# A transformer block with a recurrent time mix: when its weight chunks are loaded and split, where y is transposed, and the form of its recurrence

## The chip, the cores and the metric

One core of a Trainium2 chip runs the whole kernel. The metric is the device time of one execution in microseconds; the median of three runs is quoted. The five engines that take part are TensorE (PE), VectorE (DVE), ScalarE (ACT), GpSimd (POOL) and SyncE (SP), which issues most of the DMAs. Each runs its own instructions in the order in which they were recorded and waits for the others by semaphores.

## The reference

One layer, 1024 tokens of width 1024, all in float32:

```python
x = x + 0.5 * swiglu(rms_norm(x, ffn1_norm), ffn1_w_gate, ffn1_w_up, ffn1_w_down)
z = rms_norm(x, mix_norm) @ w_in
z_rwkv, z_attn, z_gate = jnp.split(z, [RWKV_COLS, RWKV_COLS + ATTN_COLS], axis=-1)
y_rwkv = rwkv7_time_mix(z_rwkv, ...)
y_attn = dilated_attention_mix(z_attn, cos, sin, q_norm, k_norm)
g_rwkv, g_attn = jnp.split(jax.nn.sigmoid(z_gate), N_BRANCHES, axis=-1)
x = x + (g_rwkv * (y_rwkv @ w_br_rwkv) + g_attn * (y_attn @ w_br_attn)) @ w_out
x = x + 0.5 * swiglu(rms_norm(x, ffn2_norm), ffn2_w_gate, ffn2_w_up, ffn2_w_down)
x = x + jax.nn.sigmoid(rms_norm(x, ple_norm) @ ple_w_gate) * (p_i @ ple_w_proj)
```

The change touches the time mix and the attention's beginning. The time mix shifts z by one token, makes r, k, v, a decay w, a rate a and a gate g of it, and runs, for each of 8 heads of 64, a state of 64 x 64 through the 1024 tokens: `state = state * w + sa (kk * a) + v k`, with `sa = -state kk`, and `y = state r`. y is then normalised per head, gets a bonus term and is multiplied by g. The attention has three groups of four heads, each with its own window and dilation.

## The kernel before, in words

Every large product is made of three float32r products (`mm3`, L265 to L267), since weights and activations are split into a high and a low part. A weight chunk of 128 x 1024 is loaded by `wchunk` (L252 to L260): a DMA into a staging tile `wst` (two buffers), then ScalarE writes the high part of a `wsp` tile (three buffers; L249) and GpSimd the low part (L250). All users of the mixer draw on these two rings in turn.

The mixer (`mixer`, L1872) has two stages. In the first, `rwkv` (L845), the time mix goes through 8 units: 4 pairs of heads, each in two halves of 512 tokens. A unit has three steps, written as generators:

- `zstage` (L922): three z blocks (k, r, v) of 24 dense products each; each begins with its own `zw` chunk.
- `wkv_a` (L968), `wkv_b` (L1140): decay and keys (`QR`, `BK`), scores of keys with keys and queries (L1055), the inverse of a triangular matrix in blocks (`X` on VectorE, L1119 and L1121; L1182 to L1212 on TensorE), then a recurrence over 8 chunks of 64 tokens. A step of it (L1247 to L1266) makes two products of QR with the state S (L1254, one per head, 64 x 64), a subtraction on VectorE (L1258), two products with BKn (L1263), and a state update on VectorE (L1264).
- `wkv_c` (L1282): y out of the accumulators (`psy`, whose last products are L1278), its norm (`rsqrt`, L237 to L243, small operations of VectorE), gain, bias and bonus on GpSimd (L1319 to L1324), the product with g on VectorE (L1326), then four transposes on TensorE (L1329) and the store of y (L1332).

In the second stage the queries and keys of a head group are normalised and rotated (`qk_post`, L1474), then the attention core runs (`attn_core`, L1544): per block of 128 queries the scores (L1575), mask and maximum on VectorE (L1579), the exponentials on ScalarE (L1585), transposes (L1597) and the products with v (L1618).

What sets the order is `weave` (L112): it records the instructions of several streams into one program by a simple clock of its own. A stream tells with each `yield` how long its piece keeps TensorE busy and how long it then has to wait, as `yield 0, 8.0` ahead of y's transposes (L1325). Streams marked "F" are dense products, which fill the gaps: first `zstage`, then a filler of gate blocks (`gates`, L1350) and the first attention projection (`qkv_first`, L1430). What of the filler is not used up in the first stage goes on in the second, beside `qkv_gemm` (L1440), whose next projection waits until `qk_post` is done with the last.

## Time and profile before

| what | us |
|---|---|
| median of 3 runs | 2735.73 |
| lowest and highest run | 2727.03, 2739.34 |
| the profiled execution, its own time | 2731.04 |
| its span, first to last instruction | 2729.3 |
| TensorE busy in the span | 2518.9 (92%) |
| VectorE, ScalarE, GpSimd busy | 1586.2, 973.2, 1148.3 |
| mean granted clock of TensorE | 0.961 |

A busy time is the time in which an engine had an instruction in work. TensorE's instructions overlap, so its busy time is not all work at its peak. The granted clock is the share of the full TensorE clock that the chip allowed. A float32 product on TensorE stands in the trace as two passes, a float32r product and a transpose as one.

### The profile page before, as it was taken

Reading aid. Unit: us, or ns where it says so; the run is one execution under the profiler, and the core shown is the slowest. Engines: PE = TensorE matmul, PEld = TensorE weight load, DVE = VectorE, ACT = ScalarE, POOL = GpSimd, SP = SyncE. Lnnn points to the kernel's source line nnn. Section 1 sums busy time; section 2 is a strip of 40 time slices with the busy share of each in tenths; the row PEclk is TensorE's granted clock in tenths of the full one; section 3 lists DMA queues with packets and bytes.
Section 4 is the critical chain, followed back from the end, with each engine's and each line's share of the span. In section 5 each row is a group of like instructions: output and inputs, shape, how many; then the busy total and the mean of one; then the engine's idle time right before and its main releaser. Section 6 shows DMA issues by size and latency. Waiting matters only on the chain.

```text
span 2729.3 us, 37026 instructions
## 1 busy us (share of the span) xinstructions
PE 2518.9 (92%) x14541; PEld 2038.0 (75%) x14541; DVE 1586.2 (58%) x2519; ACT 973.2 (36%) x1700; POOL 1148.3 (42%) x635
## 2 busy tenths in 40 slices
PE   6899999899999999889989998879799999989899
PEld 5688888777777666667877998658578888768677
DVE  4865556788715555554356325382876556677852
ACT  5433333333434323332224343421533332333541
POOL 2675556555424333332222212150565655555540
PEclk9899999999999999999989999899899999999999
DMA  5222222736333222222231101572132222453532
GB/s 187 93 85 70 93 78 93 282 120 211 129 117 91 60 62 56 62 60 59 76 113 43 63 32 43 180 210 113 46 99 82 88 77 93 147 222 110 180 121 93
DMA packets 272498, 289.18 MB, mean 106 GB/s; under 512 B 46282, under 2 KB 202540, under 8 KB 272068
## 3 DMA queue, kind: packets, MB, share of 16 engines
q1 hardware_dynamic: 264932, 274.59, 30.7%
q10 hardware_dynamic: 7392, 12.23, 1.3%
q8 instruction: 114, 1.87, 0.3%
q14 instruction: 60, 0.49, 0.1%
HBM read 222.64 MB, written 64.14 MB: 105 GB/s over the span
## 4 chain that ended last, share of the span: by engine, by line
PE 48%; DVE 13%; POOL 3%; issue 2%; DMA 2%; ACT 2%; SPq 0%; ACTq 0%; DVEq 0%; POOLq 0%
PE g L265 7%; PE g L266 6%; PE g L267 6%; PE dn L266 6%; PE dn L267 6%; PE dn L265 5%; PE tr L267 1%; PE tr L265 1%; PE tr L266 1%; POOL wsp L250 1%; PE t L1055 1%; PE s L1575 1%; DMA fb<-f 1%; DVE sub L1119 1%; PE pt L1597 1%
## 5 line engine op out<-in xcount | busy, mean ns | idle before, releaser
L250 POOL TENSOR_TENSOR wsp<-wr,wsp 128x1024 fp32r<-128x1024 f32 (+1 forms) x158 | 361.5, 2296 | 374.4 <-ACT wsp L249 334.2
L250 POOL TENSOR_TENSOR wsp<-wst,wsp 128x1024 fp32r<-128x1024 f32 x71 | 173.4, 2445 | 425.2 <-ACT wsp L249 372.4
L250 POOL TENSOR_TENSOR wsp<-ws,wsp 128x1024 fp32r<-128x1024 f32 x88 | 222.0, 2524 | 212.0 <-ACT wsp L249 210.3
L265 PE MATMUL g<-h,wsp 128*128 128x512 f32 x496 | 220.7, 445 | 12.2 <-DVE h L1714 10.6
L265 PE MATMUL g<-wsp,h 128*128 128x256 f32 (+1 forms) x664 | 217.0, 327 | 16.0 <-ACT raw L1427 10.2
L267 PE MATMUL g<-wsp,h 128*128 128x256 f32 (+1 forms) x664 | 207.6, 313 | 0.0
L266 PE MATMUL g<-wsp,h 128*128 128x256 f32 (+1 forms) x664 | 207.5, 313 | 0.0
L267 PE MATMUL g<-h,wsp 128*128 128x512 f32 x496 | 201.3, 406 | 0.0
L266 PE MATMUL g<-h,wsp 128*128 128x512 f32 x496 | 201.0, 405 | 0.0
L407 DVE TENSOR_TENSOR ws<-wr 128x512 f32<-128x512 f32 x56 | 86.6, 1554 | 166.8 <-POOL x L250 165.4
L249 ACT ACTIVATE wsp<-ws 128x1024 fp32r<-128x1024 f32 (+1 forms) x110 | 106.4, 968 | 191.6 <-PE dn L267 74.4
L249 ACT ACTIVATE wsp<-wr 128x1024 fp32r<-128x1024 f32 (+1 forms) x158 | 133.7, 851 | 107.6 <-DVE wr L751 42.5
L265 PEld LDWEIGHTS g<-wsp,h 128*128 128x128 f32 x664 | 138.5, 209 | 28.2 <-ACT raw L1427 10.9
L265 PE MATMUL dn<-wsp,h 128*128 128x512 f32 x360 | 143.8, 405 | 13.5 <-DVE x L792 6.9
L266 PE MATMUL dn<-wsp,h 128*128 128x512 f32 x360 | 143.7, 399 | 7.9 <-POOL wsp L250 7.9
L267 PE MATMUL dn<-wsp,h 128*128 128x512 f32 x360 | 142.1, 396 | 0.7 <-DVE h L250 0.6
L266 PEld LDWEIGHTS g<-wsp,h 128*128 128x128 f32 x664 | 139.0, 209 | 3.7 <-issue 0.2
L267 PEld LDWEIGHTS g<-wsp,h 128*128 128x128 f32 x664 | 138.6, 209 | 3.7
L463 DVE TENSOR_TENSOR act<-act,m 128x512 f32<-128x512 f32 x88 | 130.7, 1485 | 1.4
L265 PEld LDWEIGHTS g<-h,wsp 128*128 128x128 f32 x496 | 96.5, 194 | 44.0 <-DVE h L1714 11.6
L267 PE MATMUL dn<-h,wsp 128*128 128x512 f32 x320 | 124.6, 389 | 0.0
L265 PE MATMUL dn<-h,wsp 128*128 128x512 f32 x320 | 124.5, 389 | 0.0
(467 smaller groups left out, 6604.6 us busy)
## 6 DMA issues: line engine op xcount, KB each, us to landing
wr<-ffn_w_down SPq DMA_DIRECT2D x44, 1024.0 KB
wst<-w_in SPq DMA_DIRECT2D x60, 512.0 KB
wr<-ffn_w_gate SPq DMA_DIRECT2D x44, 512.0 KB
wr<-ffn_w_up SPq DMA_DIRECT2D x44, 512.0 KB
actD<-act SPq DMA_DIRECT2D x44, 512.0 KB
a<-actD SPq DMA_DIRECT2D x12, 1024.0 KB
gate<-gst SPq DMA_DIRECT2D x26, 256.0 KB
wst<-ffn_w_down SPq DMA_DIRECT2D x10, 512.0 KB
```

The costliest lines, as they stand in the source:

```text
L249: nc.scalar.activation(dst[:, 0], src, AF.Copy)
L250: (lo_eng or nc.vector).tensor_tensor(out=dst[:, 1], in0=src, in1=dst[:, 0].bitcast(F32), op=ALU.subtract)
L265: mm(ps, lhsT=l[0], rhs=r[0], start=first, stop=False)
L266: mm(ps, lhsT=l[0], rhs=r[1], start=False, stop=False)
L267: mm(ps, lhsT=l[1], rhs=r[0], start=False, stop=last)
L407: self.nc.vector.tensor_tensor(out=out, in0=R[:, i], in1=R[:, j], op=op)
L463: eng.tensor_tensor(out=a, in0=a, in1=v, op=ALU.mult)
L1055: PE.matmul(psd[h][:, i2, e].rearrange("p (a s) -> p a s", a=2), lhsT=BK[hr, i, 2 * e:2 * e + 2].rearrange("p a s -> p (a s)"), rhs=QR[hr, ...
L1119: V.tensor_tensor(out=pr[:, :s + 1, :n], in0=XT[:, :s + 1, s:s + 1].to_broadcast([64, s + 1, n]), in1=at[:, s:s + 1, s + 1:].to_broadcast( ...
L1575: PE.matmul(ps[h][:, pr, :nk * P], lhsT=qT[hr, pr, j * P:(j + 1) * P], rhs=kT[hr, pr, k0:k0 + nk * P], start=True, stop=True)
L1597: PE.transpose(pt[:, h], S[:, h, kt * P:(kt + 1) * P], self.ident)
```

## The change

- Loads and splits of a weight chunk are two calls now, `wload` and `wsplit`. The staging tiles are `wst0` and `wst1`, the split ones `wsp0`, `wsp1`, `wsp2`, each with one buffer; the z blocks use `wst0` and, in turn, `wz` and `wsp0`, the filler `wst1`, `wsp1` and `wsp2`.
- A z block's load is issued when the block before it begins, and its split stands after the fourth of that block's eight pieces. The filler (`fill`, in place of `qkv_first` and the gates ahead of it) does the same.
- The recurrence's two products of 64 x 64 per head become one of 128 x 128 for both: the state is kept as a block-diagonal tile `Sbd` of 128 x 128, whose off-diagonal blocks are zero. The state update on VectorE becomes two, one for each head. The time that a step is said to take on TensorE is 0.11 in place of 0.16, and its second wait 0.7 in place of 0.5.
- y's product with g, transposes and store come after a wait of 14.0 in place of 8.0.
- The scratch for DMAs is smaller (1024), which frees memory.

```diff
@@ class K
-    def wchunk(self, src, kdim, pool=None, tag="wsp", bufs=3):
...
-        st = self.t(self.wp, [P, 1024], "wst", bufs=2)
-        nc.sync.dma_start(st[:, :n].rearrange("p (k n) -> p k n", k=kdim), src)
-        sp = self.t(pool or self.wp, [P, 2, 1024], tag, dt=F32R, bufs=bufs)
-        self.split(sp[:, :, :n], st[:, :n], lo_eng=nc.gpsimd)
+    def wchunk(self, src, kdim, pool=None, tag=None, bufs=1):
+        return self.wsplit(self.wload(src, kdim), pool, tag, bufs)
+    def wst(self, q=None):
+        if q is None:
+            q = self.wq = 1 - self.wq
+        return self.t(self.wp, [P, 1024], f"wst{q}")
+    def wload(self, src, kdim, q=None):
         n = kdim * src.shape[-1]
+        st = self.wst(q)
+        self.nc.sync.dma_start(st[:, :n].rearrange("p (k n) -> p k n", k=kdim), src)
+        return st, kdim, n
...
+    def wsplit(self, load, pool=None, tag=None, bufs=1):
+        st, kdim, n = load
+        sp = self.t(pool, [P, 2, 1024], tag, dt=F32R, bufs=bufs) if pool else self.wsp(tag)
+        self.split(sp[:, :, :n], st[:, :n], lo_eng=self.nc.gpsimd)
@@ def rwkv: zstage, sz
             for x in (1, 0, 2):
-                W = zw(4 * x + hb)
+                if not zready:
+                    zsplit()
+                W = zready.pop()
+                if zorder:
+                    nextz.append(zload(zorder.pop(0)))
                 d = zt[x, hb, hf] = self.t(sp, [P, HALF], f"z{x}{hf}")
-                yield from zblock(4 * x + hb, W, hf, d)
+                for n, r in enumerate(zblock(4 * x + hb, W, hf, d)):
+                    yield r
+                    if n == 3 and nextz:
+                        zsplit()
...
+        def zsplit():
+            zslots.append(zslots.pop(0))
+            zready.append(self.wsplit(nextz.pop(), *zslots[0]))
@@ def wkv_b
-                for h in range(2):
-                    hr = slice(64 * h, 64 * h + 64)
-                    PE.matmul(pu[ur[e], h, 256:320], lhsT=QR[hr, i, qs], rhs=S[hr, cc], start=True, stop=True)
-                yield 0.16, 0.5
-                SP = self.t(sp, [P, 64], "SP", bufs=2)
+                PE.matmul(U2, lhsT=QR[:, i, 0:2].rearrange("p a s -> p (a s)"), rhs=S[:, cc], start=True, stop=True)
+                yield 0.11, 0.5
+                SP = self.t(sp, [P, P], "SP", bufs=2)
                 A.activation(SP, S[:, cc], AF.Copy, scale=pcol)
                 V.tensor_tensor(out=UV[ur[e], i, e].rearrange("p (h s) -> p h s", h=2),
...
+                PE.matmul(dS, lhsT=BKn[:, i, e], rhs=UV[:, i, e], start=True, stop=True)
                 for h in range(2):
                     hr = slice(64 * h, 64 * h + 64)
-                    PE.matmul(pu[hr, 0, 320:384], lhsT=BKn[:, i, e, hr], rhs=UV[:, i, e, hr], start=True, stop=True)
-                V.scalar_tensor_tensor(out=S[:, cc + 1], in0=pu[:, 0, 320:384], scalar=pcol, in1=SP, op0=ALU.mult,
-                                       op1=ALU.add)
-                yield 0.16, 0.5
+                    V.scalar_tensor_tensor(out=S[hr, cc + 1, hr], in0=dS[hr, hr], scalar=pcol[hr], in1=SP[hr, hr],
+                                           op0=ALU.mult, op1=ALU.add)
+                yield 0.11, 0.7
@@ def wkv_c
-        yield 0, 8.0
+        yield 0, 14.0
         V.tensor_tensor(out=yc, in0=yc, in1=gs, op=ALU.mult)
@@ def mixer
         def fill():
-            yield from take(gates, max(NFIRST - gates0, 0) * 16)
-            yield from self.qkv_first(hT, mx, D_["raw"])
+            yield from self.fill(hT, mx, D_["gate"], D_["raw"], range(gates0, NFIRST))
             done.add("raw0")
-            yield from gates
+            yield from self.gates(hT, mx, D_["gate"], range(NFIRST, 16))
```

Line numbers of the changed kernel are some 40 higher in these parts: its L1097 is L1055 of before, L1233 and L1235 are L1191 and L1193, L1368 is L1329, and L284 to L286 are L265 to L267.

On TensorE, third unit, around the four transposes of y (`yc`): before,

```order
L1182 MATMUL t_1342_8315<-TT_8157,SC_7697 64x32 x4
L265 MATMUL g_8276<-h_864_5453,wsp_8272 128x512
L266 MATMUL g_8276<-h_864_5453,wsp_8272 128x512
L267 MATMUL g_8276<-h_864_5453,wsp_8272 128x512
L1182 MATMUL t_1342_8315<-TT_8157,SC_7697 64x32 x8
L1329 MATMUL t_1343_8340<-cst_p_66,yc_8126 128x128 x4
L1055 MATMUL t_1346_8349<-QR_8252,BK_8253 128x128
```

and now,

```order
L1235 MATMUL t_1357_8392<-TT_8138,N_884_5614 64x32 x2
L284 MATMUL g_8323<-h_868_5475,wsp_1264_7847 128x512
L285 MATMUL g_8323<-h_868_5475,wsp_1264_7847 128x512
L286 MATMUL g_8323<-h_868_5475,wsp_1264_7847 128x512
L1097 MATMUL t_1355_8386<-QR_8294,BK_8295 128x128
L1097 MATMUL t_1356_8387<-QR_8294,BK_8295 128x128
L1368 MATMUL t_1358_8444<-cst_p_66,yc_8212 128x128 x4
```

The transposes stood ahead of all scores of the keys; now six of these and the first part of the inverse stand ahead of them. The count of dense products between the unit's last y product (L1278) and the transposes went from 54 to 57, and to the first scores from 54 to 45.

On VectorE, the same unit, around y's product with g (L1326, third row from the end; in the changed kernel L1365, second from the end): before,

```order
L1318 TENSOR_TENSOR yc_8126<-yc_8126,grsy_8197 128x512
L1016 TENSOR_SCALAR n_1329_8246<-t_1327_8237 128x8
L1017 RECIPROCAL n_1329_8246<-n_1329_8246 128x8
L1014 SCALAR_TENSOR_TENSOR ta_8174<-ta_8174,kk_8214 128x512
L1028 SCALAR_TENSOR_TENSOR BK_8253<-ta_8174,iP_8217 128x4x128
L1030 TENSOR_TENSOR BK_8253<-z_1202_7480,iP_8217 128x4x2x64
L1326 TENSOR_TENSOR yc_8126<-yc_8126,gsl_8123 128x512
L888 SCALAR_TENSOR_TENSOR z_1319_8192<-g_8193,omu_5597,zu_8266 128x512
L1185 TENSOR_TENSOR N_882_5609<-t_1342_8315,cst_r_5592 128x16x16
```

and now,

```order
L1056 SCALAR_TENSOR_TENSOR ta_8225<-ta_8225,kk_8240 128x512
L243 SCALAR_TENSOR_TENSOR grsy_8263<-grsu_8264,grsy_8263 128x8
L1072 TENSOR_TENSOR BK_8295<-z_1195_7395,iP_8243 128x4x2x64
L1070 SCALAR_TENSOR_TENSOR BK_8295<-ta_8225,iP_8243 128x4x128
L1357 TENSOR_TENSOR yc_8212<-yc_8212,grsy_8263 128x512
L1365 TENSOR_TENSOR yc_8212<-yc_8212,gsl_8209 128x512
L1227 TENSOR_TENSOR N_884_5614<-t_1351_8356,cst_r_5597 128x16x16
```

The two operations that make BK stand ahead of both large operations on y now (in two other units of before, y's product stood ahead of them).

On TensorE, at the end of the first attention core, where its statistics (`ast`) are transposed: before,

```order
L1597 MATMUL pt_12578<-cst_p_66,S_12528 128x128 x4
L267 MATMUL g_12524<-h_860_5431,wsp_12396 128x512
L1553 MATMUL pt_12588<-cst_p_66,ast_11991 8x128 x4
L1618 MATMUL po_12437<-PT_12571,vt_11726 64x128
L1553 MATMUL pt_12594<-cst_p_66,ast_11991 8x128 x4
L1618 MATMUL po_12437<-PT_12571,vt_11726 64x128 x3
L1618 MATMUL po_12438<-PT_12571,vt_11726 64x128 x4
L265 MATMUL g_12524<-h_862_5442,wsp_12396 128x512
L266 MATMUL g_12524<-h_862_5442,wsp_12396 128x512
L267 MATMUL g_12524<-h_862_5442,wsp_12396 128x512
```

and now,

```order
L285 MATMUL g_12694<-wsp_1965_12664,h_809_5021 128x256
L1671 MATMUL pt_12588<-cst_p_66,S_12544 128x128 x4
L1627 MATMUL pt_12595<-cst_p_66,ast_12122 8x128 x4
L1692 MATMUL po_12478<-PT_12581,vt_11857 64x128
L1692 MATMUL po_12479<-PT_12581,vt_11857 64x128
L1627 MATMUL pt_12601<-cst_p_66,ast_12122 8x128 x4
L1692 MATMUL po_12478<-PT_12581,vt_11857 64x128 x3
L1692 MATMUL po_12479<-PT_12581,vt_11857 64x128 x3
L1589 MATMUL pt_12645<-cst_p_66,rt_1956_12621 128x128 x4
```

The gate products (128 x 512) between and behind the core's steps are gone; products of the next projection (128 x 256) stand between its last steps.

## Rows read from the trace of the kernel before

**Rows 1.** Busy time by stretch: us, then each engine's, granted clock, DMA share, GB/s.
```profile
812.00:1403.00 591.00, 546.40 (x5255) 417.46 (x5256) 301.13 (x720) 187.10 (x378) 193.03 (x154) 0.94 0.24 66
1403.00:1442.00 39.00, 28.08 (x181) 26.69 (x182) 29.10 (x60) 9.93 (x17) 8.37 (x4) 0.82 0.41 137
1442.00:1528.00 86.00, 80.81 (x485) 60.36 (x486) 41.13 (x122) 38.20 (x101) 18.62 (x8) 0.94 0.18 62
```

**Rows 2.** Waits of TensorE, 812 to 1403: total us, times, longest.
```profile
PE t L1329 <- DVE yc L1326: 24.0, 7, 7.2
PE t L1055 <- ACT wsp L249: 6.2, 2, 3.3
...
PE t L1055 <- DVE BK L1028: 2.9, 2, 2.3
```

**Rows 3.** Timeline, second unit: start, us, engine, line, tiles, [idle before <- releaser].
```profile
990.01 1.15 PE L1278 MATMUL st<-UV,SC 128*64 128x64 f32 x32
...
1013.76 1.76 DVE L1028 SCALAR_TENSOR_TENSOR BK<-ta,iP 128x512 f32<-128x512 f32 x1
...
1015.67 1.20 PE L1055 MATMUL t<-QR,BK 64*128 64x128 f32 x4 [3.33 <-ACT wsp L249]
```

**Rows 4.** Busy time in slices of 10 us, columns as in rows 1.
```profile
1010.00:1020.00 10.00, 4.96 (x29) 4.10 (x30) 6.52 (x6) 3.79 (x7) 6.73 (x6) 0.63 0.27 82
1020.00:1030.00 10.00, 10.00 (x107) 7.42 (x105) 2.04 (x4) 0.36 (x1) 0.00 (x0) 0.69 0.28 80
...
1120.00:1130.00 10.00, 8.45 (x103) 5.45 (x102) 8.12 (x34) 2.66 (x6) 1.40 (x2) 1.00 0.19 54
...
1280.00:1290.00 10.00, 7.19 (x95) 6.26 (x90) 4.97 (x5) 1.29 (x3) 4.70 (x4) 0.78 0.25 81
```

**Rows 5.** Timeline, third unit, around the transposes of y.
```profile
1059.95 1.15 PE L1278 MATMUL st<-UV,SC 128*64 128x64 f32 x32
...
1061.37 0.40 PE L266 MATMUL g<-h,wsp 128*128 128x512 f32 x1
1061.61 0.39 PE L267 MATMUL g<-h,wsp 128*128 128x512 f32 x1
...
1073.56 0.69 DVE L1318 TENSOR_TENSOR yc<-yc,grsy 128x512 f32<-128x512 f32 x1
...
1074.48 1.66 DVE L1014 SCALAR_TENSOR_TENSOR ta<-ta,kk 128x512 f32<-128x512 f32 x1
...
1075.68 1.61 POOL L1320 TENSOR_TENSOR yc<-yc,gn 128x512 f32<-128x512 f32 x1
...
1079.00 1.75 DVE L1030 TENSOR_TENSOR BK<-z,iP 128x512 f32<-128x512 f32 x1 [1.16 <-POOL z L1012]
1080.67 1.75 DVE L1326 TENSOR_TENSOR yc<-yc,gsl 128x512 f32<-128x512 f32 x1
...
1082.56 1.08 PE L1329 MATMUL t<-cst_p,yc 128*128 128x128 f32 x4 [3.86 <-DVE yc L1326]
```

**Rows 6.** Timeline of TensorE, a step of the recurrence.
```profile
1038.87 0.33 PE L1254 MATMUL st<-S,QR 64*64 64x64 f32 x4
1039.14 0.66 PE L1099 MATMUL t<-cst_p,z 128*128 128x128 f32 x4
1039.63 0.95 PE L1108 MATMUL t<-rki,kk 128*128 128x2 f32 x8
```

**Rows 7.** One line's instructions: count, duration in ns min/median/max, first and last start.
```profile
L1264 DVE SCALAR_TENSOR_TENSOR S<-st,PC,SP x64: 269/284/285, 902.9 to 1381.2; 128x64 f32<-128x64 f32 x64
```

**Rows 8.** Groups by line, 812 to 1403: xcount | busy us, mean ns | idle before, releasers.
```profile
L1055 PE MATMUL t<-QR,BK 64*128 64x128 f32 x256 | 27.4, 316 | 9.3 <-ACT wsp L249 6.2 <-DVE BK L1028 2.9 <-ACT Qn L1159 0.2
```

**Rows 9.** Waits of SP's queue, 812 to 1403: total us, times, longest.
```profile
SPq L1295 <- DVE yc L1326: 63.3, 7, 11.1
```

**Rows 10.** Timeline of TensorE, scores of the first attention core.
```profile
1456.48 2.76 PE L1575 MATMUL s<-qkT,qkT 64*128 64x256 f32 x8 [2.82 <-DVE ast L1579]
...
1498.45 1.14 PE L1575 MATMUL s<-qkT,qkT 64*128 64x256 f32 x8
...
1504.80 1.13 PE L1575 MATMUL s<-qkT,qkT 64*128 64x256 f32 x8
```

More of the change, by code (lines that the diff above doesn't have):

```diff
@@ L409, in st_slot @@
     def st_slot(self):
-        return self.t(self.wp, [P, 2, 1024], "wsp", dt=F32R, bufs=3).rearrange("p s (c f) -> p s c f", c=2)
+        return self.wsp().rearrange("p s (c f) -> p s c f", c=2)
     def st_mm(self, ps, op, f, first, last):
@@ L870, in rwkv @@
         nc.gpsimd.memset(N1, 0.0)
+        Sbd = [self.t(sp, [P, 9, P], f"Sbd{q}") for q in range(2)]
+        for q in range(2):
+            nc.gpsimd.memset(Sbd[q], 0.0)
         carry = self.t(self.cp, [P, 14], "carry")
@@ L957, in sc @@
                 done.add(("c", u))
+        zorder = [4 * x + hb for hb, hf in units for x in (1, 0, 2)]
+        nextz, zready, zslots = [], [], [(sp, "wz"), (None, 0)]
+        def zsplit():
+            zslots.append(zslots.pop(0))
+            zready.append(self.wsplit(nextz.pop(), *zslots[0]))
         def sz():
+            nextz.append(zload(zorder.pop(0)))
             for u in range(8):
@@ L1351, in gates @@
         for b in blocks:
-            W = self.gate_w(b)
+            c0 = GATE0 + b * P
+            W = self.wsplit(self.wload(self.a["w_in"][:, c0:c0 + P].rearrange("(k p) n -> p k n", p=P), KB, 1), None, 1 + b % 2)
             for hf in range(2):
@@ L1355, in gates, with fill, get @@
                 yield from self.gate(hT, W, b, hf, gD, st, hf == 0)
+    def fill(self, hT, sp, gD, rawD, blocks):
+        w_in = self.a["w_in"]
+        gsrc = lambda b: (w_in[:, GATE0 + b * P:GATE0 + (b + 1) * P].rearrange("(k p) n -> p k n", p=P), KB)
+        qsrc = lambda x, b: (w_in[b * 512:(b + 1) * 512, ATTN0 + 768 * x:ATTN0 + 768 * x + 256]
+                             .rearrange("(k p) n -> p k n", p=P), 4)
+        srcs = [gsrc(b) for b in blocks] + [qsrc(x, b) for x in range(3) for b in range(2)]
+        load = lambda: self.wload(*srcs.pop(0), 1) if srcs else None
+        free = self.ffree = [1, 2]
+        def get():
+            nonlocal raw
+            q = free.pop(0)
+            W = self.wsplit(raw, None, q)
+            raw = load()
+            return W, q
+        raw = load()
+        cur = get()
+        for b in blocks:
+            for hf in range(2):
+                st = self.t(sp, [P, HALF], "gst2", bufs=2)
+                for n, r in enumerate(self.gate(hT, cur[0], b, hf, gD, st, hf == 0)):
+                    yield r
+                    if hf and n == 1:
+                        nxt = get()
+            free.append(cur[1])
+            cur = nxt
+        cur = [cur, get()]
+        for x in range(3):
+            W = [w for w, q in cur]
+            nxt = []
+            for i in range(NT):
+                st = self.t(sp, [P, HALF], "gst2", bufs=2)
+                yield from self.qkv_tile(hT, W, slice(i * P, (i + 1) * P), st[:, 0:256], True)
+                self.nc.sync.dma_start(rawD[x, :, i], st[:, 0:256])
+                if 3 <= i < 6 and x < 2 and free and not nxt:
+                    nxt.append(get())
+            free.extend(q for w, q in cur)
+            while x < 2 and len(nxt) < 2:
+                nxt.append(get())
+            cur = nxt
+            yield 0, 0
     def rope(self, sp, ta, tb):
@@ L1428, in qkv_tile @@
         yield 0.65, 0, more
-    def qkv_first(self, hT, sp, rawD):
-        for x in range(3):
-            W = self.qkv_weights(0, x)
-            for i in range(NT):
-                st = self.t(sp, [P, HALF], "gst2", bufs=2)
-                yield from self.qkv_tile(hT, W, slice(i * P, (i + 1) * P), st[:, 0:256], True)
-                self.nc.sync.dma_start(rawD[x, :, i], st[:, 0:256])
-            yield 0, 0
     def qkv_gemm(self, hT, sp, sp1, env, vD):
```

45 lines of the change are left out of this document (25 added, 20 removed).

## The prediction

> **What bounds the kernel now.** I first cut the span by stage [rows 1]. The time mix runs from 812 to 1403 us. TensorE is busy 546.4 of these 591 us, VectorE 301, ScalarE 187 and GpSimd 193, so TensorE sets the pace: 44.6 us of idling, and a granted clock of 0.94, are what there is to win. In the next 39 us VectorE is busy 29.1 and TensorE 28.1: there the queries and keys of the first head group are normalised, and VectorE's chain sets the pace. In the 86 us after that TensorE is busy 80.8 again; the first attention core runs there, with gate products between its steps.
>
> Second, who TensorE waited for in the time mix [rows 2]. The transposes of y (L1329) cost 24.0 us in 7 waits, the scores of the keys (L1055) 9.1 in 4. No product of a z block waits for a weight chunk. One row blames ScalarE's `wsp` for L1055, which does not read it; in the timeline [rows 3] BK, which it does read, is finished by VectorE at 1013.76 + 1.76 = 1015.52, and L1055 starts at 1015.67. So both waits are for VectorE's queue, in which y's last product (L1326) stands next to the products that make BK (L1014, L1028, L1030).
>
> Third, the clock around one such wait [rows 4]: 5.04 us idle and a clock of 0.63 (a mix of the two levels, 1.2 and 2.4 GHz) in one slice, full work at 0.69 in the next. That is (0.37 + 0.31) x 10 = 6.8 us, less some 2.5 that fell on idle time: 4.3 of work lost. Six of seven units show such a pair, 26 us in all. The slice at 1120 idles 1.55 us and keeps 1.00; the one at 1280 idles 2.81 and falls to 0.78.
>
> **The change part by part.**
>
> *Chunks ahead, own slots.* No wait of rows 2 goes with this: 0 us. The load and both halves of the split are the same instructions, earlier in SP's, ScalarE's and GpSimd's queues. Its cover is half a block of other products; were it gone, each first product would wait for a split.
>
> *What the reordering feeds TensorE.* By the order, 52 more groups of three gate products stand in the time mix (201 for 149) and as many fewer in the attention (7 for 59). Dense products follow each other by 0.23 us (1061.37 and 1061.61 in [rows 5]): 156 x 0.23 = **+36 us** here, to be paid back later or not.
>
> *Full form.* A step's two pairs of 64-wide products become two products of 128 columns. The pair, four passes in the trace, takes 1038.87 to 1039.14, 0.27 us; the four passes of 128 columns behind it (transposes) take 0.49, so a full product, two passes, takes 0.245 [rows 6]. 128 x 0.025 = **-3 us** on TensorE. The Trainium skill, TensorEngine Tiling (Array Packing), Overview, says that small products placed on independent tiles run up to 2x faster; by it the full form would lose this, up to 0.27 us more per product, and the sum below would be 35 us higher. I go by the row. VectorE gets a second state update per step, 0.28 us each [rows 7], 64 x 0.28 = 18 us. The order puts six dense products (1.4 us) behind the step's second product where three stood, which covers it; with that cover gone it would be 0.28 per step on the path, +18. The two memsets of the wide state are GpSimd's, once, beside other work.
>
> *y transposed later.* Take the unit whose y products end at 1059.95 + 1.15 = 1061.1 [rows 5]. TensorE reached L1329 at 1082.56 - 3.86 = 1078.7, 17.6 us later. In the new order three more dense products (0.7), six products of L1055 (27.4 us over 128, 0.2 each [rows 8]: 1.3) and 32 narrow ones (an estimate of 0.1 each from the same row: 3.2) stand before it: 22.8. The first L1055 now stands ahead of y, nine dense products sooner: 17.6 - 2.1 = 15.5. That is the new wait to look for. L1014 started at 1074.48; L1318 (0.69) leaves its front, and GpSimd's L1012 is ahead of y's L1319 and L1320, so that L1030's idle 1.16 goes. From 1073.8, three operations of 1.7 us end at 1078.9, 17.8 after: L1055 waits 2.3 us here, nothing where VectorE's small operations run quicker. y then needs L1318 (0.7), three GpSimd operations of up to 1.6, and L1326 (1.75): 17.8 + 0.7 + 4.6 + 1.75 = 24.9, where TensorE stands at 22.8 + 2.3 = 25.1: no wait. I take 2 us for each of six units, 12 in place of 33: **-21 us** (bounds: -33 without any wait, 0 if L1055 takes over all of it).
>
> *Behind y.* The store of y moves with it. SP waits for L1326 before it loads g (L1295), 63.3 us in all [rows 9], and the chunk loads queue behind; 2 to 3 us later costs nothing: 27 dense products and all narrow ones of the unit's inverse stand between y and the next z block.
>
> *The clock.* 2 us lies between 1.55 (kept) and 2.81 (lowered) of rows 4, so I let two of six units lose 4.3: **-17 us** (bounds -26 and 0).
>
> Stage: 36 - 3 - 21 - 17 = **-5 us** (-26 to +33).
>
> *The attention pays back.* From 1442 to 1528 its gate products are gone; 45 products of the next projection (half the columns, so 0.12 each, 5.3 us) move in. How long does the core take bare? With dense work between, the scores of two neighbouring blocks stand 1504.80 - 1498.45 = 6.35 apart, of which the last three dense products are 0.7 [rows 10]. So 5.6 us bare, 7 x 5.6 plus a last block of 6 = 45. TensorE will be sparse and slow at times: the scores took 2.76 at 1456 where they took 1.14 at 1498, so I add 3 us to four blocks, and 3 for the keys' chain in the same VectorE queue: 60. 86 + 5 - 60 = 31, so **-31 us** (bounds: 50 and 80, so -41 to -11). The 39 us before are VectorE's and stay.
>
> **The sum.** -5 - 31 = -36 on the profiled execution's 2731.0 gives 2695. That execution lies 4.7 under the median of 2735.7, so on the median I forecast **2700 us** (2680 to 2715 with smaller errors of the same terms).
>
> **The rivals.**
> - *The clock stays up.* Waits under 1 us and no fall: stage 36 - 3 - 30 - 26 = -23, sum -54: 2682. For it: the dense work per unit grows, and the 1120 slice. Against: narrow products surround the place.
> - *The attention starves.* The core takes 80 us bare, because VectorE's 41.1 us of rows 1 interleave badly: -11, sum -16: 2720. For it: the first 39 us idle with just that chain.
> - *The wait only moves.* L1055 waits 5.5 us per unit and the clock falls as before: stage +33, attention -31: 2738.
> - *Keys later still (slower).* In the unit of rows 3, L1055 started 1015.67 - 991.16 = 24.5 after the y products. If BK comes that late everywhere, L1055, arriving at 15.5, waits 9 us: six units cost 54 in place of 33, the clock is not regained, stage +54, sum +23: 2759. Against: L1326 held VectorE's queue in that unit, and now stands behind BK. It decides from BK at about 21 us on.
> - *Packing lost.* Each full-form product takes 0.54 us, twice the pair's 0.27: 128 x 0.27 = +35, so 2735. The 0.245 of rows 6 speaks against it. This is what the rule of Array Packing named above would do.
> - *The change does nothing of what it names* for chunks is part of every case, since no chunk is waited for.
>
> **How the numbers follow.** 0.5% of 2736 is 14 us, about what a measurement can tell: faster is under 2722, slower over 2749. Forecast 0.42, clock up 0.16, attention starved 0.17 (2720 lies near the border: half counted as the same), wait moved 0.10, keys later 0.10, packing 0.05. Faster 0.42 + 0.16 + 0.09 = 0.67; same 0.08 + 0.10 + 0.05 = 0.23; slower 0.10. The range runs from both best bounds, -26 - 41 = -67 (2669), to 2748, which leaves out the slower rival.
>
> **What would show it.** Right: L1329's wait gone or under 5 us; L1055 waiting some 12; the stretch from the first L914 to the last L1329 near 586 us with more TensorE work in it; no wait of a z product for `wsp` or `wz`; the clock near 0.97 there; the stretch from the first scores to the resumed projection near 55 to 60 us with TensorE idling. Wrong: L1055 over 30 us, a core of 80 us, or a wait between the two products of a step for VectorE's second update.

## The result, and the profile after

The changed kernel takes **2772.7 us** (median of 6 runs, 2763.1 to 2780.4) where the kernel before takes 2735.2: ratio 1.0136, 95% interval 1.0120 to 1.0152. It is 37 us slower; the forecast was 2700.

The profiled execution after took 2780.4 us, 7.7 above its median, and that of before lies 4.2 below the 2735.2, so the two traces differ by 49, and 12 of these are no part of the result. Where the rest lies is read by stretches that hold the same work. Before, the first attention core (from the first scores to the first transposes of its statistics) and the stretch behind it, to the last transposes of queries and keys, read (columns as in [rows 1]):

```profile
1441.80:1511.30 69.50, 64.29 (x396) 47.04 (x396) 40.64 (x121) 32.91 (x92) 16.43 (x7) 0.93 0.14 46
...
1511.30:1694.00 182.70, 174.47 (x1210) 163.65 (x1209) 76.58 (x179) 64.94 (x155) 42.30 (x16) 0.98 0.14 48
```

After: the time mix, the 39 us of [rows 1] in which VectorE sets the pace, and the same two stretches:

```profile
823.80:1460.50 636.70, 577.01 (x5161) 465.79 (x5160) 313.46 (x784) 197.51 (x386) 196.61 (x155) 0.92 0.24 66
1460.50:1502.60 42.10, 28.10 (x194) 26.24 (x193) 29.83 (x55) 11.95 (x19) 13.87 (x6) 0.84 0.46 152
...
1502.60:1569.70 67.10, 57.91 (x331) 41.60 (x330) 41.12 (x126) 29.03 (x87) 11.88 (x5) 0.77 0.05 16
...
1569.70:1733.30 163.60, 155.39 (x1107) 146.96 (x1106) 76.66 (x179) 60.73 (x149) 37.54 (x14) 0.97 0.13 42
```

The time mix grew from 591.0 to 636.7 us. The 156 dense products that it draws in are 36 of these; TensorE idles 59.7 us where 44.6 stood, and its clock is 0.92 where it was 0.94. The attention pays back 2.4 + 19.1 - 3.1 = 18, not 31: its core idles 9.2 us at a clock of 0.77.

Who TensorE waits for in the time mix, after (answers to [rows 2]):

```profile
PE t L1233 <- issue: 19.7, 5, 6.2
PE st L1293 <- DVE Sbd L1303: 8.6, 5, 2.1
PE t L1097 <- DVE BK L1070: 7.6, 4, 4.1
PE t L1097 <- ACT Qn L1201: 6.9, 2, 4.2
PE st L1300 <- DVE UV L1297: 6.9, 12, 2.0
...
PE t L1097 <- DVE BK L1072: 2.3, 1, 2.3
```

The transposes of y (L1368 now) wait for nothing any more. In their place stand the first step of the inverse (L1233, 19.7), the scores of the keys (L1097, 16.8) and the steps of the recurrence (L1293 and L1300, 15.5; their lines of before waited 4.6). One row names no releaser ("issue"); the timeline of its longest wait, all engines, shows it:

```profile
967.75 1.77 DVE L1072 TENSOR_TENSOR BK<-z,iP 128x512 f32<-128x512 f32 x1
969.06 2.68 POOL L250 TENSOR_TENSOR wz<-wst,wz 128x1024 fp32r<-128x1024 f32 x1
969.44 2.85 DVE L1357 TENSOR_TENSOR yc<-yc,grsy 128x512 f32<-128x512 f32 x1
...
972.37 1.26 POOL L1358 TENSOR_TENSOR yc<-yc,gn 128x512 f32<-128x512 f32 x1 [0.63 <-DVE yc L1357]
...
976.35 0.69 DVE L1365 TENSOR_TENSOR yc<-yc,gsl 128x512 f32<-128x512 f32 x1 [4.05 <-POOL yc L1363]
976.96 0.41 DVE L1227 TENSOR_TENSOR N<-t,cst_r 128x256 f32<-128x256 f32 x1
...
977.47 0.41 PE L1233 MATMUL t<-N,TT 64*64 64x32 f32 x3 [6.22 <-issue]
```

L1233 reads N. N's product on VectorE takes 0.41 us, but stands behind y's product with g (L1365), which waits 4.05 us for y's three products on GpSimd, and these start when VectorE has ended L1357. N ends at 977.37 and L1233 starts at 977.47; in all five waits it starts 0.10 us after N. The wait for y has not gone; TensorE meets it at the inverse.

L1357 takes 2.85 us here, begun while GpSimd splits a chunk (969.06 + 2.68), and mostly 0.69:

```profile
L1357 DVE TENSOR_TENSOR yc<-yc,grsy x8: 676/688/2848, 969.4 to 1444.4; 128x512 f32<-128x512 f32 x8
```

The same stands in the trace of before, around y's product with g:

```profile
L1326 DVE TENSOR_TENSOR yc<-yc,gsl x8: 693/2284/2833, 944.4 to 1398.9; 128x512 f32<-128x512 f32 x8
...
1008.68 2.34 POOL L250 TENSOR_TENSOR wsp<-wst,wsp 128x1024 fp32r<-128x1024 f32 x1
...
1008.75 2.81 DVE L1326 TENSOR_TENSOR yc<-yc,gsl 128x512 f32<-128x512 f32 x1 [3.13 <-POOL yc L1324]
```

In seven units it begins while an operation of GpSimd runs, takes 1.75 to 2.83 us, and L1329 waits; in the eighth nothing runs on GpSimd, it takes 0.69, and L1329 does not wait. Together the seven take 11.7 us more than they would at 0.69, beside 24.0 us of waits at L1329. No run tests this cause by itself.

The second loss is at the stage's start, in a place that no wait of before pointed to. Timelines of TensorE, ScalarE, GpSimd and SP, after:

```profile
787.27 0.50 PE L284 MATMUL g<-h,wz 128*128 128x512 f32 x1 [1.68 <-ACT wz L249]
...
789.71 0.80 PE L286 MATMUL g<-h,wz 128*128 128x512 f32 x1 [1.47 <-POOL wz L250]
...
819.30 0.50 PE L284 MATMUL g<-h,wsp 128*128 128x512 f32 x1 [1.72 <-ACT wsp L249]
...
819.36 2.35 POOL L250 TENSOR_TENSOR wsp<-wst,wsp 128x1024 fp32r<-128x1024 f32 x1
...
821.74 0.38 SPq L265 DMA_DIRECT2D wst<-w_in  x1
...
821.76 0.50 PE L286 MATMUL g<-h,wsp 128*128 128x512 f32 x1 [1.73 <-POOL wsp L250]
...
848.07 1.06 ACT L249 ACTIVATE wsp<-wst 128x1024 fp32r<-128x1024 f32 x1 [4.08 <-DMA wst<-w_in]
```

Twice, for the first chunk (`wz`) and for the first z chunk (in `wsp0`, which the second chunk holds until then), TensorE waits 3.2 to 3.5 us for the two halves of a split. And all z chunks now pass through one staging tile, so the next load is issued (821.74) when GpSimd has ended the split before it (819.36 + 2.35). A chunk then takes some 7.5 us from load to load, and a z block 24 x 0.23 = 5.5: ScalarE stands 4.08 us before a split, with the other work of its queue behind it.

### The profile page after: what moved, and what is told of

Its sections match the earlier page's. It is cut to its first block, busy times and chain, and to the rows that moved or that the text cites. A ratio compares the mean times of both kernels' runs of the same rounds, so it can differ in the third digit from the quotient of the medians.

```text
span 2778.6 us, 36586 instructions
## 1 busy us (share of the span) xinstructions
PE 2536.9 (91%) x14285; PEld 2072.6 (75%) x14285; DVE 1613.5 (58%) x2583; ACT 977.5 (35%) x1700; POOL 1136.5 (41%) x637
## 4 chain that ended last, share of the span: by engine, by line
PE 39%; DVE 9%; issue 3%; DMA 2%; POOL 2%; ACT 1%; SPq 0%; ACTq 0%; DVEq 0%; POOLq 0%
PE g L284 5%; PE dn L285 5%; PE dn L286 5%; PE dn L284 5%; PE g L286 5%; PE g L285 5%; PE tr L285 1%; PE tr L286 1%; PE tr L284 1%; POOL wsp L250 1%; PE s L1649 1%; DMA wr<-ffn_w_down 1%; PE pt L1671 1%; PE po L1692 1%; DVE ws L770 1%
## 5 line engine op out<-in xcount | busy, mean ns | idle before, releaser
L250 POOL TENSOR_TENSOR wsp<-wr,wsp 128x1024 fp32r<-128x1024 f32 (+1 forms) x158 | 349.2, 2218 | 392.7 <-ACT wsp L249 343.4
L250 POOL TENSOR_TENSOR wsp<-wst,wsp 128x1024 fp32r<-128x1024 f32 x58 | 141.7, 2446 | 369.7 <-ACT wsp L249 251.2
L284 PE MATMUL g<-wsp,h 128*128 128x256 f32 (+1 forms) x664 | 217.4, 327 | 13.2 <-DVE m L543 8.2
L286 PE MATMUL g<-wsp,h 128*128 128x256 f32 (+1 forms) x664 | 209.3, 315 | 0.0
L284 PE MATMUL g<-h,wsp 128*128 128x512 f32 x384 | 173.6, 452 | 20.5 <-DVE h L1788 16.4
L286 PE MATMUL g<-h,wsp 128*128 128x512 f32 x384 | 159.2, 415 | 3.5 <-POOL wsp L250 3.5
L285 PE MATMUL g<-h,wsp 128*128 128x512 f32 x384 | 160.2, 417 | 0.0
L284 PEld LDWEIGHTS g<-wsp,h 128*128 128x128 f32 x664 | 140.0, 211 | 23.8 <-DVE m L543 9.0
L284 PE MATMUL dn<-wsp,h 128*128 128x512 f32 x360 | 143.6, 404 | 11.6 <-DVE x L811 6.0
L286 PE MATMUL dn<-wsp,h 128*128 128x512 f32 x360 | 143.6, 400 | 1.2 <-DVE h L250 1.0
L286 PEld LDWEIGHTS g<-wsp,h 128*128 128x128 f32 x664 | 139.6, 210 | 4.6 <-issue 1.0
L286 PE MATMUL dn<-h,wsp 128*128 128x512 f32 x320 | 124.6, 389 | 0.0
L284 PE MATMUL dn<-h,wsp 128*128 128x512 f32 x320 | 124.5, 389 | 0.0
L285 PE MATMUL dn<-h,wsp 128*128 128x512 f32 x320 | 124.5, 389 | 0.0
```

The lines of the kernel that those rows point to most:

```text
L250: (lo_eng or nc.vector).tensor_tensor(out=dst[:, 1], in0=src, in1=dst[:, 0].bitcast(F32), op=ALU.subtract)
L284: mm(ps, lhsT=l[0], rhs=r[0], start=first, stop=False)
L285: mm(ps, lhsT=l[0], rhs=r[1], start=False, stop=False)
L286: mm(ps, lhsT=l[1], rhs=r[0], start=False, stop=last)
```

## The experiments

All eighteen runs, against the kernel before on the same chip:

| run | median us | ratio | 95% interval |
|---|---|---|---|
| the change | 2772.7 | 1.0136 | 1.0120 to 1.0152 |
| only_y_later | 2737.7 | 1.0003 | 0.9992 to 1.0014 |
| only_full_form | 2746.5 | 1.0042 | 1.0027 to 1.0057 |
| no_full_form | 2762.1 | 1.0106 | 1.0091 to 1.0121 |
| y_not_later | 2764.5 | 1.0111 | 1.0096 to 1.0126 |
| slots_swapped | 2750.6 | 1.0054 | 1.0034 to 1.0074 |
| two_staging | 2756.3 | 1.0070 | 1.0043 to 1.0097 |
| slots_and_staging | 2743.9 | 1.0037 | 1.0026 to 1.0049 |
| form_old_times | 2742.2 | 1.0029 | 1.0019 to 1.0040 |
| y_on_gpsimd | 2732.0 | 0.9994 | 0.9984 to 1.0003 |
| keys_own_buffers | 2737.1 | 1.0009 | 0.9998 to 1.0020 |
| keys_free_y_early | 2738.4 | 1.0014 | 1.0000 to 1.0028 |
| keys_free | 2721.1 | 0.9947 | 0.9933 to 0.9961 |
| kf_y_early | 2720.3 | 0.9953 | 0.9935 to 0.9970 |
| kf_form | 2707.5 | 0.9910 | 0.9894 to 0.9926 |
| kf_form_new_times | 2705.0 | 0.9889 | 0.9874 to 0.9904 |
| mended | 2725.7 | 0.9974 | 0.9958 to 0.9990 |
| mended_old_times | 2716.6 | 0.9932 | 0.9913 to 0.9951 |

### Which part costs?

**only_y_later**, the kernel before with

```diff
-        yield 0, 8.0
+        yield 0, 14.0
```

> The kernel before, with 14.0 in place of 8.0 ahead of y's transposes and nothing else. Three theories stand. Queue theory: TensorE's inverse (L1191) needs N, whose product on VectorE (L1185) stands right behind y's product with g (L1326); y's transposes (L1329) leave TensorE's path but the inverse waits for the same VectorE row in their place. It expects L1329's wait (24.0 us) nearly gone, L1191 waiting 12 us or more, and a time between 2725 and 2740 us. Form theory (the loss comes from the recurrence's full form alone): the later transposes help as forecast, L1329's wait goes and nothing of 5 us takes its place; 2695 to 2715. Filler theory (the loss comes from dense gate products drawn out of the attention): only 27 more of them stand in the time mix here (6 us), some 2 to 4 us are not paid back; with the wait gone 2705 to 2720.

No difference. Its waits of TensorE, from 780 to 1435 us:

```profile
PE t L1055 <- DVE BK L1028: 21.1, 5, 6.9
PE t L1055 <- DVE BK L1030: 5.5, 2, 3.3
...
PE t L1191 <- issue: 4.4, 2, 3.7
PE t L1055 <- ACT Qn L1159: 2.6, 2, 2.2
```

L1329 has left the list, and 33.6 us of waits stand where 24.0 + 9.1 = 33.1 stood. The inverse, where the queue theory looked, has 4.4 of it; most went to the scores of the keys.

**only_full_form**, the kernel before with the diff's recurrence, its step times and the smaller scratch:

```diff
-                    PE.matmul(pu[ur[e], h, 256:320], lhsT=QR[hr, i, qs], rhs=S[hr, cc], start=True, stop=True)
-                yield 0.16, 0.5
+                PE.matmul(U2, lhsT=QR[:, i, 0:2].rearrange("p a s -> p (a s)"), rhs=S[:, cc], start=True, stop=True)
+                yield 0.11, 0.5
...
+                yield 0.11, 0.7
```

> The kernel before, with the recurrence in full form and its new step times (0.11, 0.7), and the smaller DMA scratch; chunks and y's wait as before. 126 of the 156 dense products that the whole change draws into the time mix come with this alone, and so does BK's place ahead of y's products on VectorE. Queue theory: no split of a z chunk stands ahead of y's products on GpSimd here, so y's product with g ends sooner and the inverse (L1191) waits under 8 us in all; the steps wait 8 us more than before; 2735 to 2758 us. Form theory: the steps' waits and the state's second update carry the whole loss; 2760 to 2780. Filler theory: 126 products, 29 us in, some 12 to 16 not paid back: 2745 to 2765.

11 us slower, in the bands of two theories at once. L1329 waits 18.5, the scores 15.6 and the steps 17.0 us.

**no_full_form**, the changed kernel with the recurrence of before (the same edit, backwards).

> The changed kernel with the recurrence of before (64 x 64 products per head, its step times); chunks ahead in their own slots and y later stay. 27 dense products more than before stand in the time mix. Queue theory: VectorE's order is that of before, the splits of z chunks stand near y's products on GpSimd in some units; the first z products of the time mix still wait 3 to 6 us for their split: 2735 to 2760 us, and L1191 still waits 8 us or more. Form theory: the loss is gone: 2720 to 2738. Filler theory: 2735 to 2745, with no wait of L1191.

2762.1, over the queue theory's band and far over the form theory's; the inverse waits 6.7 us, under the 8 expected. Against only_y_later it differs by the chunks and their tiles alone (and the smaller scratch, with which keys_own_buffers, below, is no slower): **24 us**. The step that the forecast put at nothing is the largest.

**y_not_later**, the changed kernel with

```diff
-        yield 0, 14.0
+        yield 0, 8.0
```

> The changed kernel with y's wait back at 8.0; the order on VectorE and GpSimd is that of the changed kernel, y's transposes on TensorE stand earlier and 30 dense products go back to the attention. Queue theory: the wait is y's product with g behind GpSimd's split, and falls on the transposes (L1329) or on the inverse (L1191) alike; 2760 to 2785 us, the sum of both waits as in the changed kernel (20 us) or up to 10 more. Form theory and filler theory: within 5 us of the changed kernel or up to 7 below it: 2765 to 2777. If y later were itself the loss: under 2750.

8 us under the changed kernel, though the two intervals just overlap. L1368 waits 19.0 us here, L1233 hardly: the same wait in another place.

### Where the chunks cost

**slots_swapped**: no_full_form with

```diff
-        Wl = self.wsplit(self.wload(a["w_in"][:, 12 * P:13 * P]..., KB, 0), sp, "wz", 1)
+        Wl = self.wsplit(self.wload(a["w_in"][:, 12 * P:13 * P]..., KB, 0), None, 0)
...
-        Wg = zw(13)
+        Wg = self.wsplit(zload(13), sp, "wz", 1)
```

> The kernel of no_full_form (64 x 64 recurrence, chunks ahead, y later), with the first two chunks of the time mix in each other's slots: the chunk that is used first goes into wsp0, which stands in memory of its own, and the second into wz, which stands in the memory of the stage's tiles and can be written only once the stage before is done. Start theory (chunks ahead cost 24 us, from 2737.7 to 2762.1, of which 20 lie between the last gate product and the first unit's y because splits and loads of the first chunks come too late): the two waits of 3.2 and 3.4 us for a split there go, with the clock's two falls beside them: 2748 to 2757. Slot theory (the loss is in the rings that lost a buffer, all through the stage and in the merge): 2758 to 2765.

**two_staging**: also

```diff
+            zst[0] = 1 - zst[0]
+            if not zst[0]:
+                return self.wload(src, KB, 0)
+            st = self.t(sp, [P, 1024], "zst")
+            nc.sync.dma_start(st.rearrange("p (k n) -> p k n", k=KB), src)
+            return st, KB, KB * P
```

> As slots_swapped, and the z chunks are loaded into two staging tiles in turn, so that a load need not wait until GpSimd has split the chunk before it. Start theory: ScalarE, which waited 18.8 us (6 times) for chunks to land between 755 and 960 us in no_full_form, waits under 6 there, the keys' BK of the first unit is made sooner and the first scores' wait of 4.15 us goes; the first unit takes 131 to 136 us again in place of 145: 2738 to 2749. Slot theory: within 4 us of slots_swapped.

slots_swapped gains 11.5 us: the 46 us ahead of the stage take 47.6 in place of 52.6. two_staging misses its band: the second tile stands in the stage's memory, too, and the second chunk was loaded through it, which came late (waits of 4.45 and 1.70 us). Its first unit takes 132.4 us, as expected.

**slots_and_staging**: the first two chunks through the old tile, then both in turn.

```diff
-            zst[0] = 1 - zst[0]
-            if not zst[0]:
+            zst[0], zst[1] = 1 - zst[0], zst[1] + 1
+            if zst[0] or zst[1] < 3:
```

> slots_swapped and two_staging put together rightly: the first two chunks go through the old staging tile, only the z blocks' chunks alternate with the second one (in two_staging the second chunk's load had to wait for the stage's memory: 4.45 and 1.70 us at its product, and a fall of the clock). Start theory: 47 to 48 us from the last stretch before the stage to the first gate product's end as in slots_swapped (46.1 without chunks ahead) and 131 to 134 us for the first unit as in two_staging; 2739 to 2748 in all, so that 16 us or more of the 24 are explained. Slot theory: 2750 or more.

2743.9: of 24 us, 18 are back. Two stretches (the last 46 us before the time mix's first product L914; from there to the end of the first unit's last y products) in only_y_later, then no_full_form, then slots_and_staging:

```profile
751.80:797.90 46.10, 45.98 (x219) 37.88 (x217) 10.34 (x24) 16.61 (x26) 9.75 (x12) 1.00 0.41 122
797.90:929.30 131.40, 122.88 (x869) 89.73 (x869) 54.93 (x120) 50.47 (x96) 42.89 (x33) 0.97 0.28 80
```

```profile
752.30:804.90 52.60, 49.34 (x219) 39.74 (x217) 10.51 (x24) 17.56 (x27) 12.26 (x13) 0.94 0.39 117
804.90:949.90 145.00, 130.73 (x869) 94.00 (x869) 56.15 (x119) 51.71 (x96) 43.12 (x33) 0.92 0.26 72
```

```profile
752.90:803.70 50.80, 47.87 (x219) 38.91 (x217) 10.54 (x24) 17.88 (x27) 12.06 (x13) 0.97 0.44 131
803.70:936.80 133.10, 122.93 (x869) 90.04 (x869) 54.72 (x119) 50.55 (x96) 43.31 (x33) 0.97 0.28 79
```

The first unit loses 13.6 us with the chunks ahead, 5.7 of it idle and the rest at a clock of 0.92 in place of 0.97, and has 1.7 of it left with the second tile. The stretch ahead misses its band: 50.8 us, 4.7 over only_y_later, where 47 to 48 were expected. ScalarE's wait for loads into `wsp` chunks in these 200 us goes from 3.8 us to 18.8 and back to 4.0.

### What TensorE waits for in a unit

**form_old_times**: only_full_form with

```diff
-                yield 0.11, 0.5
+                yield 0.16, 0.5
...
-                yield 0.11, 0.7
+                yield 0.16, 0.5
```

> As only_full_form, but with the step times of before (0.16 and twice 0.5), so that the order draws no more dense products into the time mix than before (1058, where only_full_form has 1184). Filler theory (the 11 us of only_full_form are 29 us of products drawn in, of which some 18 came back): 2728 to 2738. Form theory (the steps themselves wait longer, 14.7 us in only_full_form where 4.6 were before, for two state updates in place of one): 2740 to 2750, with 10 us or more of waits at the two products of a step.

9 us slower without any product drawn in: the filler theory is wrong. The form theory's band holds it, and the steps wait 11.0 us, 6.4 more than before, as it expected; but more comes at another place, the transposes of y:

```profile
PE t L1329 <- DVE yc L1326: 38.6, 7, 7.8
```

The seven units from the first y to the last, before and here:

```profile
923.50:1383.70 460.20, 423.85 (x4356) 324.94 (x4354) 234.97 (x583) 137.84 (x285) 142.33 (x116) 0.93 0.23 62
...
926.90:1389.40 462.50, 412.85 (x4122) 331.59 (x4122) 251.90 (x633) 140.30 (x285) 141.85 (x116) 0.91 0.22 61
```

TensorE is busy 11.0 us less and idles 13.3 more.

**y_on_gpsimd**: only_y_later with

```diff
-        V.tensor_tensor(out=yc, in0=yc, in1=gs, op=ALU.mult)
+        G.tensor_tensor(out=yc, in0=yc, in1=gs, op=ALU.mult)
```

> As only_y_later, with y's product with g done by GpSimd behind its own products on y, in place of VectorE, so that neither BK nor N stands behind it on VectorE. TensorE waited 33 us for this chain in before, in only_y_later, in only_full_form and in the changed kernel alike, at four different places. Queue theory (VectorE's queue, held by y's product while that waits for GpSimd, sets it): the waits of L1055 and L1191 fall from 33.1 to under 20 us in all, 2715 to 2730. Rival (GpSimd itself, or BK's own chain, sets it): the waits stay within 6 us of 33, or grow, as GpSimd's 1.3 us more per unit stands ahead of the next work: 2733 to 2745.

Between the two bands. L1191's wait is gone, L1055's is still 28.9 us: BK is late by itself. In its second unit k (L1012) stands on GpSimd behind all of y's products and a split, and ScalarE's f (L1011) behind the load of gn.

**keys_own_buffers**: only_y_later with

```diff
-                gn = self.t(sp, [P, 2, P], "gn", bufs=2)
+                gn = self.t(sp, [P, 2, P], "gn", bufs=4)
```

> As only_y_later, with four buffers for the norm's gain and bias (gn) in place of two (and the smaller DMA scratch, for room). In the units that begin a pair of heads the load of gn is issued in ScalarE's queue and waits until GpSimd has used the old one in y's products (4.6 us in y_on_gpsimd at 1007.4 to 1012.0), and f (L1011), which k (L1012) and ta (L1014) need, stands behind it. Chain theory (BK's own inputs are late, not VectorE's queue): L1055's wait falls from 28.7 to 15 to 24 us; 2728 to 2736. Queue theory: L1055 unchanged within 3 us, 2734 to 2740.

No difference, and L1055 waits 29.4 us: gn alone is not the cause.

**keys_free**: y_on_gpsimd with the four buffers and

```diff
-        G.tensor_tensor(out=k, in0=k, in1=f, op=ALU.mult)
+        V.tensor_tensor(out=k, in0=k, in1=f, op=ALU.mult)
```

> As y_on_gpsimd, with four buffers for gn as in keys_own_buffers, and k times f (L1012) done by VectorE in place of GpSimd, where it stood behind y's products and a chunk's split. Nothing of y is then ahead of what BK or N need, on any engine. Chain theory: the waits of L1055 fall from 28.2 to under 12 us and the clock falls for a shorter time in most units; 2708 to 2724. If they stay above 20 us, something else on VectorE (the small operations of y's norm, which stand ahead) sets BK: 2726 to 2736.

2721.1, 0.53% under the kernel before. The seven units from the first y to the last, and its longest wait:

```profile
928.60:1373.80 445.20, 419.68 (x4356) 323.02 (x4354) 235.23 (x582) 137.93 (x285) 147.10 (x117) 0.95 0.23 63
```

```profile
PE t L1055 <- DVE BK L1028: 20.5, 7, 4.1
```

In only_y_later the same stretch took 458.5 us at a clock of 0.93; TensorE was busy 420.2 us in it, hardly more than here, so the gain is idle time. The wait fell less than expected (20.5, not under 12, and so where the rival had it), the time as the chain theory expected.

**keys_free_y_early**: the kernel before with the four buffers and k on VectorE (the edit of keys_free); y's product stays on VectorE, its wait 8.0.

> The kernel before, with y's wait of 8.0 and y's product with g on VectorE as they were, four buffers for gn and k times f on VectorE. Chain theory: BK is ready sooner and ahead of y's products in more units, L1055's wait (9.1 us) goes, but y's transposes (L1329), which stand early here, still wait for GpSimd's products on y: 15 to 25 us in all; 2718 to 2732. If y's place alone decided, as the change has it, keys_free would be faster than this by 15 us or more; if the waits only add up, by 5 to 12.

**kf_y_early**: keys_free with `yield 0, 8.0` in place of `yield 0, 14.0`.

> keys_free with y's wait back at 8.0. If y later is worth what the forecast said once the keys are free, y's transposes wait 20 us or more here and the time is 8 to 15 us above keys_free: 2729 to 2736. If the waits only change places, L1329 takes over what L1055 waited in keys_free (20.9 us) and the time is within 4 us of it: 2717 to 2725.

The waits for y, in keys_free_y_early and in kf_y_early:

```profile
PE t L1329 <- DVE yc L1326: 25.9, 6, 6.6
```

```profile
PE t L1329 <- POOL yc L1326: 19.6, 6, 5.2
```

Taking k away from GpSimd alone (with the four buffers) brings nothing; both must be apart. Then y's place does not matter: 2721.1 and 2720.3, L1055 waiting 20.5 us in the one and L1329 19.6 in the other.

### The parts put together

**kf_form**: keys_free with only_full_form's recurrence, at the step times of before (0.16, 0.5, 0.5).

> keys_free with the recurrence in full form at the step times of before (0.16 and twice 0.5). Steps theory: each step waits for the state's second update; the steps' waits grow from 4 to 8 us or more and the time by 5 to 10 us: 2726 to 2732. Queue theory of the form (form_old_times lost 9 us because y's transposes waited 37.1 us where 22.5 were before, behind products on VectorE that were reordered): with y and the keys apart nothing is left of it, and the form is within 3 us: 2717 to 2724.

It is not within 3 us but **13.6 faster** than keys_free by the medians (10 by the ratios, as the two ran on two chips). The same seven units, and TensorE around a step, in kf_form:

```profile
932.00:1360.50 428.50, 401.42 (x4124) 324.46 (x4122) 247.44 (x632) 140.61 (x285) 145.18 (x117) 0.95 0.24 65
```

```profile
1099.46 0.40 PE L265 MATMUL g<-h,wsp 128*128 128x512 f32 x1
1099.69 0.40 PE L1254 MATMUL st<-Sbd,QR 128*128 128x128 f32 x2
1099.84 0.48 PE L266 MATMUL g<-h,wsp 128*128 128x512 f32 x1
1100.16 0.39 PE L267 MATMUL g<-h,wsp 128*128 128x512 f32 x1
```

and in keys_free:

```profile
1105.32 0.40 PE L267 MATMUL g<-h,wsp 128*128 128x512 f32 x1
1105.65 0.33 PE L1254 MATMUL st<-S,QR 64*64 64x64 f32 x4
1105.91 0.51 PE L265 MATMUL g<-h,wsp 128*128 128x512 f32 x1
1106.25 0.40 PE L266 MATMUL g<-h,wsp 128*128 128x512 f32 x1
```

From the start of the dense product ahead to that of the second one behind are 0.70 us in the one and 0.93 in the other; two dense products are 0.46 of each. A pair of 64-wide products so costs 0.47 here and not 0.27: the dense product ahead takes 0.33 in place of 0.23 until the pair starts, the first one behind 0.34. Over all places in the two traces with a dense product of 128 x 512 ahead and two behind, outside the stretches of lower clock and without an idle wait ahead of the pair or product, the means are 0.47 us for the pair (78 places) and 0.32 for the full product (73). Seven units have 112 of them: 112 x 0.147 = 16.5, and the stretch is 16.7 shorter, with 18.3 less busy and 1.6 more idle time of TensorE. The Trainium skill, TensorEngine Tiling (Array Packing), Tiling Modes, says that a change of the tiling mode drains the array; the rows agree in that the dense products beside a pair lose 0.21 us in the mean, but those beside a full product, which changes no mode, lose 0.12 too.

**kf_form_new_times**: kf_form with the edit of form_old_times backwards (0.11, 0.5 and 0.11, 0.7).

> kf_form with the changed kernel's step times (0.11, 0.5, 0.7): 129 dense products move from the attention into the time mix (1213 for 1084). Payback as the forecast has it (the first core runs bare in 55 to 60 us): 30 us in and 25 to 30 back: 2705 to 2713. If the core stays at 67 us as in the changed kernel and clock falls there take the rest: 2714 to 2724.

**mended**: the changed kernel with slots_swapped's edit, y's product on GpSimd and k on VectorE.

> The whole changed kernel with three edits: the first two chunks in each other's slots (as slots_swapped), y's product with g on GpSimd and k times f on VectorE (as keys_free). Start and chain theories: 10 to 12 us come back at the start (slots_swapped against no_full_form) and 12 to 15 in the units (keys_free against only_y_later): 2744 to 2752, with L1191's wait of 20.0 us under 5. If the drawn-in gate products or the form decide, the waits go but the time stays above 2757.

**mended_old_times**: mended with the step times of before.

> mended with the step times of before (0.16 and twice 0.5): 129 dense products go back into the attention. If the products drawn in are paid back (as the 57 us of the first core in mended suggest), within 4 us of mended: 2722 to 2730, and the 15 to 20 us between it and kf_form are the chunks' part (start and merge). If they are not paid back: 2710 to 2719, with only 3 to 11 us left for the chunks.

kf_form_new_times, at 2705.0, is the best of all, 31 us under the kernel before. The 129 products drawn in come back there: its first core takes 60.8 us where kf_form's takes 68.6:

```profile
1443.70:1504.50 60.80, 53.58 (x330) 39.21 (x331) 39.04 (x122) 28.89 (x87) 11.83 (x5) 0.83 0.06 18
```

In mended it takes

```profile
1462.00:1519.40 57.40, 48.72 (x330) 35.85 (x330) 40.91 (x126) 29.00 (x87) 11.85 (x5) 0.88 0.06 19
```

57.4, with the same count of products that took 67.1 at a clock of 0.77 in the changed kernel; TensorE idles 8.7 us in the one and 9.2 in the other, so the difference goes with the clock. mended is 47 us faster than the changed kernel where 21 to 29 were expected. That the full form shows its worth here too, once y and the keys are apart, would account for the rest, but no run takes the form out of mended. mended_old_times is 9 us faster still, in the band of products that are not paid back: without chunks ahead they are, with them not wholly, and why stays open. It lies 6 to 9 us above kf_form (by the ratios and by the medians): what the chunks ahead still cost with the slots swapped, if the two buffers of gn, which mended keeps, cost nothing.

## Why the prediction was wrong

**Chunks ahead: "0 us", with "half a block of other products" as cover.** This is the step that failed most: 24 us (no_full_form against only_y_later). I looked for waits of before that the change could remove, found none, and took the cover from the steady state. The start has none: the first chunk's new slot `wz` stands in memory that the stage before still uses, the first z chunk waited for a slot in use (`wsp0`), and one staging tile makes loads, splits and products a chain of 7.5 us against blocks of 5.5. 18 of the 24 came back with slots and staging set right. The rest is not settled. In slots_and_staging the start is still 4.7 us longer and the first unit 1.7. And from the attention's last product with v to the first with w_out it takes 57.4 us at a clock of 0.91 in only_y_later, 62.8 at 0.86 in no_full_form and 60.7 at 0.85 in slots_and_staging.

**y later: "2 us for each of six units", -21.** It was 0 (only_y_later), or some 8 lost beside the other two parts (y_not_later). Three things failed. BK was not ready where I put it: L1055 alone waited 29 us in only_y_later. For this term the rival in which the wait only moves was right: it had 5.5 us for each of six units, 33 in all. Second, I followed y's product with g to its own reader, the transposes, and not to the work behind it on VectorE. The order rows ahead of the prediction show N right behind L1365; the inverse needs N, so L1233 took over 19.7 us. Third, I took 1.75 us as the length of L1326 and 1.7 for each operation of the keys, as they stood in one unit; L1326 takes 0.69 where nothing runs on GpSimd beside it, and L1030 0.68 in five of eight units. The sum of these waits hardly moved (33.1, 33.6, and 19.7 + 16.8 = 36.5 in the changed kernel); that it falls only when y's and the keys' products are both taken apart on VectorE and GpSimd is shown by keys_free against y_on_gpsimd and by kf_y_early against keys_free_y_early. How much of it is the order in the two queues, and how much that operations of the two engines slow each other, is not shown.

**The clock: -17.** No wait went, so nothing came back: 0.92 for 0.94. In keys_free, where waits shrank, it rose to 0.95 over the units, but TensorE's busy time did not fall with it. The condition was not met, and the price is not shown.

**Full form: -3 by the row's price, and 0.28 "covered".** In the change's setting it cost 9 to 11 us; with queues apart it gains 10 to 14. The price was too small: 0.15 us a pair and not 0.025, since the dense products on both sides of a pair slow down, which [rows 6] hides, where transposes follow the pair. The sign flipped because TensorE's saved time came back as waits (11.0 us less busy and 13.3 more idle in form_old_times). The steps' waits, which I put at nothing, grew from 4.6 to 11.0 at the old step times and to 15.5 in the change. The rival of the packing lost, twice 0.27 per product, is refuted: the full product is the cheaper one (0.32 for 0.47).

**+36 drawn in.** As forecast: 156 products at 0.23. **Paid back: -31.** Measured 18 in the changed kernel. The bare core of 60 us was right as a time of the work (57.4 in mended, 60.8 in kf_form_new_times), but at the clock that the changed kernel had there it took 67.1, inside the bounds given (50 to 80).

**The slower rival** named the keys' BK as the one place; beside it stood the inverse, the steps and the start, and the start, which no rival held, was the largest. The range's upper end, 2748, is not the sum of the worst bounds, which is 2758 (+33 and -11); the measured time lies beyond both.

## What to carry to other kernels

Before a load or a split is called hidden, walk its first few uses, not its steady state: which memory its slot shares, how many staging tiles it passes, and whether load, split and copy together are shorter than the work they hide behind. When a waiting instruction is moved, list what stands behind it in its own engine's queue and who needs that; a wait that comes out of a chain over two engines keeps its length wherever TensorE meets it, until the chain itself is shortened. A saving beside such a chain shows only once the chain is cut: the full form cost 11 us with it and gained 10 to 14 without. And the length of an operation read in one place holds for that place: see what its neighbours, and the other engines, did at the time.
